# Eleven taps of the second block's depthwise convolution go to ScalarE and GpSimd

## The chip, the cores and the metric

One core of one Trainium2 chip runs the whole program. The metric is device time in microseconds (us) for one execution, inputs and outputs in device memory. TensorE (PE) multiplies matrices, VectorE (DVE), ScalarE (ACT) and GpSimd (POOL) work elementwise, SyncE (SP) issues most transfers. Each engine works its instructions off in a fixed order and waits on semaphores for the others.

## What is computed

Two transformer blocks on 512 tokens of width 1024, in float32. The second block ("block 2") projects its normalised input once, and among other things feeds a Conformer convolution and a sparse attention ("NSA"), whose outputs are concatenated:

```python
def conformer_conv(a, b, w_dw, b_dw, ln_g, ln_b):
    u = a * jax.nn.sigmoid(b)
    y = lax.conv_general_dilated(
        u, w_dw[:, None, :], window_strides=(1,), padding=[(CONV_KERNEL - 1, 0)],
        dimension_numbers=('NWC', 'WIO', 'NWC'), feature_group_count=CONV_WIDTH_2)
    y = layernorm(y + b_dw, ln_g, ln_b)
    return jax.nn.silu(y)
...
    y_conv = conformer_conv(conv_a, conv_b, ...)
    y_nsa = nsa_mixer(q, k_c, v_c, k_s, v_s, k_w, v_w, gate_logits, ...)
    h = h + jnp.concatenate([y_conv, y_nsa], axis=-1) @ w_out[l]
    h = h + memory_attention(...)
    h = h + peer(...)
```

The convolution is depthwise and causal: each of 512 channels has its own 31 weights ("taps"), and output token t is the sum over d = 0 to 30 of weight(30 - d) times u(t - d). It runs over 4 channel groups of 128.

## The kernel before, in words

Activations lie transposed, channels on the 128 partitions and 512 tokens along the free dimension. A weight goes to TensorE as two halves: `load` (L165) brings it by DMA (`raw`), ScalarE rounds it to the high half (`whi`, L181), VectorE subtracts to get the low half (`wlo`, L182). `mm3` (L213) makes three matmuls of each product (L216 to L218). `split` (L220) does the same high and low pair for activations (ScalarE L224, VectorE L225).

`mix2` (L919) is the stage of the change. Its first part, `front`, mixes several generators: `conv2_in` (L1009) projects one channel group j of the convolution and leaves u in `x[j]` (VectorE L1020, L1023 and L1024); `compress` (L1241) makes compressed keys and values of 32-token blocks; `nsa_kv` makes keys and values; `nsa_q` makes the queries, `x[4]` to `x[7]`. Keys and queries pass `rope` (L1074): ScalarE writes the high half `roph` (L224), VectorE the low half `ropl` (L225), TensorE multiplies both with a permutation (L1081, L1082), VectorE combines (`rops` L1084, then L1085, L1086). The second part runs `nsa` (scores, softmax, values), `memory_kv`, and what is left of the convolution, interleaved.

`conv2` (L1027) is the convolution of one group. It works in place on a buffer `cy`: the first tap is a `tensor_scalar` (L1033), the next 29 are one VectorE `scalar_tensor_tensor` each (L1035: shifted u times weight, plus `cy`), each followed by a `yield`; then ScalarE adds the bias (L1037) and VectorE the last tap, writing `x[j]` (L1038). The generator `taps` in `mix2` hands out one step of it per step of `front`, so that taps lie between other VectorE work. `conv2_norm` (L1041) needs all four groups.

The order on each engine is made when the program is built: the framework takes the instructions with their written order as priority and places them by its own estimate of durations. So a change of `conv2` shifts its neighbours on every engine too. Pools with a number of buffers (`bufs`) make a writer wait until the reader of the buffer's old content is done.

In the second half of `compress`, the tile `cX` has a single buffer: GpSimd clears its padding (L1268), then ScalarE and VectorE fill it (L224, L225), then TensorE multiplies (L1279, L1280).

Of the kernel before, what the change touches and what calls it, by code (L numbers as in the profile page):

```python
# [7 lines left out]
F32 = mybir.dt.float32  # L8
# [4 lines left out]
AF = mybir.ActivationFunctionType  # L13
OP = mybir.AluOpType
# [3 lines left out]
T = 512  # L18
# [5 lines left out]
MAGIC = 12582912.0  # L24

TD = 384
GS = 16
NGS = TD // GS

# [109 lines left out]
class Kern:  # L139
# [887 lines left out]
    def conv2(self, P, u, j):  # L1027

        nc = self.nc
        y = P.tile([128, T], F32R, name="cy", bufs=3).bitcast(F32)  # L1030
        cw = lambda i: self.v2(W_CW + j * 31 + i)
        nc.vector.memset(y[:, :1], 0.0)
        nc.vector.tensor_scalar(y[:, 1:], u[:, :T - 1], cw(29), None, op0=OP.mult)  # L1033
        for d in range(2, 31):
            nc.vector.scalar_tensor_tensor(y[:, d:], u[:, :T - d], cw(30 - d), y[:, d:], op0=OP.mult, op1=OP.add)  # L1035
            yield
        nc.scalar.activation(y, y, AF.Identity, bias=self.v2(W_CB + j))  # L1037
        nc.vector.scalar_tensor_tensor(u, u, cw(30), y, op0=OP.mult, op1=OP.add)  # L1038
        yield

# [473 lines left out]
    def peer(self):  # L1514
# [3 lines left out]

        self.gd = self.dp.tile([128, NGS, 128, GS], F32, name="gd")
        self.hd = [self.dp.tile([128, 8, TD], F32, name=f"hd{i}") for i in range(16)]  # L1520
        g = self.v2(W_PN, 8)
        with ExitStack() as es:
# [3 lines left out]

            hg = B.tile([128, 2, 8 * TD], F32, name="hg")
            lists = [{} for _ in range(4)]
# [6 lines left out]
            with ExitStack() as e1:  # L1535
# [20 lines left out]
                for n, _ in enumerate(hid):  # L1556
                    next(front, None)
                    for _ in range(1 + (n % 8 == 0)):
                        if done < TD // 4 and "T" in lists[1 + done // 32]:
                            next(gts)  # L1560
                            done += 1
                        elif done == TD // 4 and not pre:
                            pre = self.dense_load(hg, 0)
# [5 lines left out]
                for j in range(2):  # L1569
                    t = B.tile([128, 128, GS], F32, name="gst", bufs=2).rearrange("p k t -> p (k t)").bitcast(F32R)  # L1570
                    acts.append(self.dense_act(pre, j, t[:, :TD], t[:, TD:2 * TD]))
            with ExitStack() as e2:
# [195 lines left out]
    def gate_matrix(self, P, B, lists):  # L1768
# [3 lines left out]
        for n in range(0, TD, 4):  # L1772
            lt = lists[1 + n // 128]["T"]
            if n % GS == 0:
                st = B.tile([128, 128, GS], F32, name="gst", bufs=2)
            o1 = P.tile([128, 4, 128], F32, name="o1", bufs=2)
# [7 lines left out]
            for t in range(4):  # L1784
                nc.tensor.matmul(ps[:, t * 128:t * 128 + 128], o2[:, t], o1[:, t], start=True, stop=True)
            nc.scalar.activation(st[:, :, n % GS:n % GS + 4], ps.rearrange("p (t k) -> p k t", t=4), AF.Copy)
            if n % GS == GS - 4:
# [216 lines left out]
```

## Time and profile before

| | |
|---|---|
| three executions | 4443.55, 4454.96 (median), 4459.59 us |
| the profiled execution | 4446.65 us, of which the span is 4444.8 us |
| TensorE busy | 4278.3 us, 96% |
| VectorE busy | 2896.4 us, 65% |
| ScalarE busy | 2084.4 us, 47% |
| GpSimd busy | 474.1 us, 11% |
| convolution's taps, L1035 | 116 instructions, from 2624.9 to 2820.1 us |

The spans count from the start of the profiled execution. A share over the whole span is a mean over stages with different limits; the stage of the convolution is about 200 us of 4445. In the rows, PE is a matmul and PEld the weight load that overlaps it, and `cy` in a row is any buffer of that name.

### The profile page before, as it was taken

Reading aid. Unit: us, or ns where it says so; the run is one execution under the profiler, and the core shown is the slowest. Engines: PE = TensorE matmul, PEld = TensorE weight load, DVE = VectorE, ACT = ScalarE, POOL = GpSimd, SP = SyncE. Lnnn points to the kernel's source line nnn. Section 1 sums busy time; section 2 is a strip of 40 time slices with the busy share of each in tenths; the row PEclk is TensorE's granted clock in tenths of the full one; section 3 lists DMA queues with packets and bytes.
Section 4 is the critical chain, followed back from the end, with each engine's and each line's share of the span. In section 5 each row is a group of like instructions: output and inputs, shape, how many; then the busy total and the mean of one; then the engine's idle time right before and its main releaser. Section 6 shows DMA issues by size and latency. Waiting matters only on the chain. (4 is left out here: it accounts for less than half of the span.)

```text
span 4444.8 us, 57315 instructions
## 1 busy us (share of the span) xinstructions
PE 4278.3 (96%) x21268; PEld 3651.0 (82%) x21268; DVE 2896.4 (65%) x5563; ACT 2084.4 (47%) x3514; POOL 474.1 (11%) x399
## 2 busy tenths in 40 slices
PE   9999999999999999998999999899989999999999
PEld 7888887788888888887878877878889999877777
DVE  5346777553444448778563469855889987566666
ACT  4225776432232236776442234843437777333333
POOL 0000111000000001110000000000043232223322
PEclk9999999999999999999999999999999999999999
DMA  4233222522322232223872333422388999988885
GB/s 142 92 102 104 89 88 76 173 100 91 110 90 95 99 114 81 96 89 111 257 236 92 102 104 116 136 100 70 115 294 308 311 328 319 324 307 299 303 298 180
DMA packets 264104, 726.97 MB, mean 164 GB/s; under 512 B 24848, under 2 KB 92944, under 8 KB 258704
## 3 DMA queue, kind: packets, MB, share of 16 engines
q1 hardware_dynamic: 226960, 589.07, 39.5%
q0 software_dynamic: 36864, 134.23, 8.5%
q8 instruction: 167, 2.74, 0.2%
q14 instruction: 113, 0.93, 0.1%
HBM read 630.94 MB, written 92.27 MB: 163 GB/s over the span
## 5 line engine op out<-in xcount | busy, mean ns | idle before, releaser
L181 ACT ACTIVATE whi<-raw 128x1024 fp32r<-128x1024 f32 (+2 forms) x814 | 810.3, 996 | 1730.8 <-PE ps_a L217 860.4
L182 DVE TENSOR_TENSOR wlo<-raw,whi 128x1024 fp32r<-128x1024 f32 (+2 forms) x814 | 931.8, 1145 | 749.3 <-ACT whi L181 746.7
L216 PE MATMUL ps_a<-xh,whi 128*128 128x512 f32 x1808 | 708.5, 392 | 17.8 <-ACT xh L227 10.2
L217 PE MATMUL ps_a<-xl,whi 128*128 128x512 f32 x1808 | 707.1, 391 | 1.8 <-DVE xl L228 1.5
L218 PE MATMUL ps_a<-xh,wlo 128*128 128x512 f32 x1808 | 706.2, 391 | 0.0
L216 PEld LDWEIGHTS ps_a<-xh,whi 128*128 128x128 f32 x1808 | 341.1, 189 | 91.2 <-ACT xh L227 11.0
L216 PE MATMUL ps_H<-xh,whi 128*128 128x384 f32 (+1 forms) x1088 | 384.0, 353 | 23.0 <-ACT hid L1674 23.0
L217 PEld LDWEIGHTS ps_a<-xl,whi 128*128 128x128 f32 x1808 | 341.3, 189 | 73.8 <-DVE xl L228 2.9
L218 PEld LDWEIGHTS ps_a<-xh,wlo 128*128 128x128 f32 x1808 | 341.3, 189 | 71.4
L216 PE MATMUL ps_P<-xh,whi 128*128 128x512 f32 (+1 forms) x952 | 381.3, 401 | 12.4 <-DVE sq L511 4.2
L218 PE MATMUL ps_P<-xh,wlo 128*128 128x512 f32 (+1 forms) x952 | 376.5, 396 | 10.1 <-DVE wlo L182 10.1
L217 PE MATMUL ps_P<-xl,whi 128*128 128x512 f32 (+1 forms) x952 | 377.9, 397 | 0.0
L218 PE MATMUL ps_H<-xh,wlo 128*128 128x384 f32 (+1 forms) x1088 | 375.8, 346 | 1.0 <-DVE wlo L182 0.9
L217 PE MATMUL ps_H<-xl,whi 128*128 128x384 f32 (+1 forms) x1088 | 375.3, 345 | 0.0
L217 PE MATMUL ps_D<-wlo,gah 128*128 128x512 f32 x756 | 302.2, 400 | 22.2 <-DVE wlo L182 22.2
L216 PE MATMUL ps_D<-whi,gah 128*128 128x512 f32 x756 | 300.4, 397 | 6.7 <-ACT whi L181 6.6
L218 PE MATMUL ps_D<-whi,gal 128*128 128x512 f32 x756 | 299.3, 396 | 0.0
L216 PE MATMUL ps_a<-ah,whi 128*128 128x512 f32 x704 | 277.5, 394 | 0.0
L218 PE MATMUL ps_a<-ah,wlo 128*128 128x512 f32 x704 | 276.0, 392 | 0.0
L217 PE MATMUL ps_a<-al,whi 128*128 128x512 f32 x704 | 273.2, 388 | 0.0
L1797 POOL DMA_INDIRECT row<-in_pu_dram,ei x128 | 166.4, 1300 | 785.9 <-DVE tk L1510 389.7
L1797 POOL DMA_INDIRECT row<-in_pv_dram,ei x128 | 201.3, 1573 | 388.3 <-DVE y L1810 238.1
(545 smaller groups left out, 8048.5 us busy)
## 6 DMA issues: line engine op xcount, KB each, us to landing
raw<-in_up_dram SPq DMA_DIRECT2D x176, 512.0 KB
raw<-in_uT_dram SPq DMA_DIRECT2D x128, 512.0 KB
raw<-in_pv_dram SPq DMA_DIRECT2D x128, 512.0 KB
raw<-in_dn_dram SPq DMA_DIRECT2D x64, 704.0 KB
raw<-in_w_qkv_dram SPq DMA_DIRECT2D x48, 512.0 KB
hd<-hid SPq DMA_DIRECT2D x128, 192.0 KB
gd<-gst SPq DMA_DIRECT2D x24, 1024.0 KB
hg<-hd SPq DMA_DIRECT2D x16, 1536.0 KB
```

The lines of the kernel that those rows point to most:

```text
L181: nc.scalar.activation(hi[:, :m], t, AF.Copy)
L182: self.last = nc.vector.tensor_tensor(lo[:, :m], t, hi[:, :m].bitcast(F32), OP.subtract)
L216: mm(ps, wh, ah, start=start, stop=False)
L217: mm(ps, wh, al, start=False, stop=False)
L218: mm(ps, wl, ah, start=False, stop=stop)
L1797: nc.gpsimd.indirect_dma_start(out=r, out_offset=None, in_=src, in_offset=bass.IndirectOffsetOnAxis(ap=li["ei"][:, s:s + 1], axis=0))
```

## The change

Shifts 20 to 30, eleven taps of each group, leave VectorE's chain. ScalarE multiplies the shifted u by its weight (an `activation` Copy with a per-channel scale): the first product goes straight into a new buffer `cz`, the other ten into `czt`, which has two buffers. GpSimd clears the first 20 columns of `cz` and adds each `czt` to it, ten `tensor_tensor` per group. VectorE's chain keeps shifts 1 to 19, and gains one add of `cz` after the bias, before the last tap. A `conv2` now has 19 steps where it had 30, so that the generator ends sooner.

```diff
+FAR = 20
...
+        z = P.tile([128, T], F32, name="cz")
+        nc.gpsimd.memset(z[:, :FAR], 0.0)
+        nc.scalar.activation(z[:, FAR:], u[:, :T - FAR], AF.Copy, scale=cw(30 - FAR))
         nc.vector.memset(y[:, :1], 0.0)
         nc.vector.tensor_scalar(y[:, 1:], u[:, :T - 1], cw(29), None, op0=OP.mult)
-        for d in range(2, 31):
+        for d in range(2, FAR):
             nc.vector.scalar_tensor_tensor(y[:, d:], u[:, :T - d], cw(30 - d), y[:, d:], op0=OP.mult, op1=OP.add)
+            if FAR + d - 1 < 31:
+                s = FAR + d - 1
+                t = P.tile([128, T], F32, name="czt", bufs=2)
+                nc.scalar.activation(t[:, s:], u[:, :T - s], AF.Copy, scale=cw(30 - s))
+                nc.gpsimd.tensor_tensor(z[:, s:], t[:, s:], z[:, s:], OP.add)
             yield
         nc.scalar.activation(y, y, AF.Identity, bias=self.v2(W_CB + j))
+        nc.vector.tensor_tensor(y, y, z, OP.add)
         nc.vector.scalar_tensor_tensor(u, u, cw(30), y, op0=OP.mult, op1=OP.add)
```

In the changed file the lines of `conv2` are: product into `cz` L1037, tap L1041, product into `czt` L1045, GpSimd's add L1046, bias L1048, VectorE's add of `cz` L1049, last tap L1050. Lines above `conv2` move by 2, lines below it by 12.

The order moves at three places that matter below. First GpSimd, in the second half of `compress` (`cX` is the padding that TensorE's next product needs). Before:

```order
L1239 MEMSET QB 64x512
L1268 MEMSET cX 128x4x24
L1322 CAST kzh<-kch 64x2x32 x4
L1122 CAST V_21784<-V_21784 128x4x64
L1122 CAST V_21814<-V_21814 128x4x64
```

Now:

```order
L1251 MEMSET QB 64x512
L1046 TENSOR_TENSOR cz<-czt,cz 128x491
L1046 TENSOR_TENSOR cz<-czt,cz 128x490
L1046 TENSOR_TENSOR cz<-czt,cz 128x489
L1046 TENSOR_TENSOR cz<-czt,cz 128x488
L1046 TENSOR_TENSOR cz<-czt,cz 128x487
L1046 TENSOR_TENSOR cz<-czt,cz 128x486
L1046 TENSOR_TENSOR cz<-czt,cz 128x485
L1046 TENSOR_TENSOR cz<-czt,cz 128x484
L1046 TENSOR_TENSOR cz<-czt,cz 128x483
L1046 TENSOR_TENSOR cz<-czt,cz 128x482
L1280 MEMSET cX 128x4x24
```

The clearing of `cX` now stands behind all ten adds of group 0.

Second ScalarE, where the keys are made (`vc` belongs to `compress`, `roph` is the keys' rope). Before:

```order
L224 ACTIVATE vc_21655<-kc 32x64 x2
L224 ACTIVATE vc_21661<-kc 32x64 x2
L181 ACTIVATE whi<-raw 128x192
L181 ACTIVATE whi<-raw 128x1024
L224 ACTIVATE roph<-cQ 128x512 x2
```

Now:

```order
L226 ACTIVATE vc_21694<-kc 32x64 x2
L1045 ACTIVATE czt<-x_64,wv 128x489
L1045 ACTIVATE czt<-x_64,wv 128x488
L1045 ACTIVATE czt<-x_64,wv 128x487
L1045 ACTIVATE czt<-x_64,wv 128x486
L183 ACTIVATE whi<-raw 128x192
L1045 ACTIVATE czt<-x_64,wv 128x485
L1045 ACTIVATE czt<-x_64,wv 128x484
L1045 ACTIVATE czt<-x_64,wv 128x483
L1045 ACTIVATE czt<-x_64,wv 128x482
L183 ACTIVATE whi<-raw 128x1024
L226 ACTIVATE roph<-cQ 128x512 x2
```

Eight products of group 1 (`x_64` is `x[1]`) now stand ahead of the keys' `roph`.

Third ScalarE, where the first two queries are made (`x_67` and `x_68` are `x[4]` and `x[5]`, `x_65` is `x[2]`). Before:

```order
L181 ACTIVATE whi<-raw 128x1024
L224 ACTIVATE roph<-x_67 128x512
L224 ACTIVATE roph<-x_68 128x512
L1236 ACTIVATE QQ<-x_67 64x512
L1161 ACTIVATE cX<-ps_S 128x512
```

Now:

```order
L183 ACTIVATE whi<-raw 128x1024
L226 ACTIVATE roph<-x_67 128x512
L1045 ACTIVATE czt<-x_65,wv 128x487
L1045 ACTIVATE czt<-x_65,wv 128x486
L1045 ACTIVATE czt<-x_65,wv 128x485
L1045 ACTIVATE czt<-x_65,wv 128x484
L226 ACTIVATE roph<-x_68 128x512
L1045 ACTIVATE czt<-x_65,wv 128x483
L1045 ACTIVATE czt<-x_65,wv 128x482
L1248 ACTIVATE QQ<-x_67 64x512
L1173 ACTIVATE cX<-ps_S 128x512
```

Four products stand between the two queries' `roph`; the product into `cz` and four more stand ahead of the first. At the third pair, `x[6]` and `x[7]`, the products of group 3 lie in the same way, and the last four stand ahead of the first softmax's exponential.

## Rows read from the trace of the kernel before

**Rows 1.** The page: each engine's busy time, share of the span, instructions.

```profile
PE 4278.3 (96%) x21268; PEld 3651.0 (82%) x21268; DVE 2896.4 (65%) x5563; ACT 2084.4 (47%) x3514; POOL 474.1 (11%) x399
```

**Rows 2.** Windows: length; busy us of PE, PEld, DVE, ACT, POOL; granted clock; DMA.

```profile
2625.00:2636.00 11.00, 10.62 (x63) 9.03 (x61) 10.52 (x15) 3.79 (x7) 0.18 (x1) 1.00 0.29 97
2636.00:2651.70 15.70, 6.86 (x35) 6.72 (x35) 15.42 (x42) 4.33 (x9) 1.85 (x4) 0.62 0.31 108
2651.70:2656.70 5.00, 4.84 (x14) 4.03 (x15) 4.84 (x13) 3.40 (x10) 0.00 (x0) 0.50 0.00 0
2656.70:2740.00 83.30, 79.80 (x386) 62.95 (x385) 81.13 (x125) 22.89 (x34) 2.53 (x5) 0.99 0.37 120
2740.00:2838.00 98.00, 89.69 (x638) 81.82 (x639) 89.85 (x253) 79.46 (x204) 3.12 (x6) 0.99 0.36 122
```

**Rows 3.** Tile `cy`: line, engine, operation, count: ns min/median/max, first and last start.

```profile
L1035 DVE SCALAR_TENSOR_TENSOR cy<-x,wv,cy x116: 639/730/754, 2624.9 to 2820.1; 128x510 f32<-128x510 f32 x4, 128x509 f32<-128x509 f32 x4, 128x508 f32<-128x508 f32 x4, 128x507 f32<-128x507 f32 x4
L1037 ACT ACTIVATE cy<-cy,wv x4: 707/710/722, 2669.9 to 2820.8; 128x512 f32<-128x512 f32 x4
L1057 DVE TENSOR_TENSOR cy<-cy,cQ x3: 681/684/686, 2832.8 to 2834.8; 128x512 f32<-128x512 f32 x3
```

**Rows 4.** Windows, instructions of L1035 alone: DVE busy us, count.

```profile
2624.00:2740.00 116.00, 57.67 (x80) 0.92 0.34 111
2740.00:2838.00 98.00, 25.68 (x36) 0.99 0.36 122
```

**Rows 5.** Lines L721 and L633: GpSimd's two-input product and its cast.

```profile
L721 POOL TENSOR_TENSOR sq<-sq,lg x16: 1288/1298/2143, 435.3 to 2068.8; 128x512 f32<-128x512 f32 x16
L633 POOL CAST KB<-KK x32: 602/612/963, 413.9 to 2045.6; 64x512 fp32r<-64x512 f32 x32
```

**Rows 6.** Timeline at 2068 us, VectorE, then GpSimd: start, length, operation.

```profile
2068.55 1.22 DVE L182 TENSOR_TENSOR wlo<-raw,whi 128x1024 fp32r<-128x1024 f32 x1
...
2068.78 2.14 POOL L721 TENSOR_TENSOR sq<-sq,lg 128x512 f32<-128x512 f32 x1 [22.56 <-DVE sq L720]
```

**Rows 7.** Timeline at 413 to 419 us, VectorE, then GpSimd.

```profile
414.16 1.11 DVE L553 SCALAR_TENSOR_TENSOR BL<-x,x,x 128x512 fp32r<-128x512 f32 x1
415.19 0.68 DVE L225 TENSOR_TENSOR vv<-ps_T,vv 128x512 fp32r<-128x512 f32 x1
415.90 1.05 DVE L630 TENSOR_TENSOR KK<-qk,KK 64x512 fp32r<-64x512 f32 x1
416.98 0.99 DVE L631 TENSOR_TENSOR QB<-qk,QQ 64x512 fp32r<-64x512 f32 x1
418.00 0.69 DVE L630 TENSOR_TENSOR KK<-qk,KK 64x512 fp32r<-64x512 f32 x1
...
413.94 0.78 POOL L633 CAST KB<-KK 64x512 fp32r<-64x512 f32 x1 [28.65 <-ACT KK L628]
...
416.47 0.96 POOL L633 CAST KB<-KK 64x512 fp32r<-64x512 f32 x1
```

**Rows 8.** Timeline of TensorE, four places; in brackets the idle time before.

```profile
2638.83 0.37 PE L1279 MATMUL ps_T<-cX,whi 128*128 128x136 f32 x1 [3.20 <-DVE cX L225]
2651.75 0.42 PE L216 MATMUL ps_P<-whi,dvh 128*128 128x64 f32 x1 [6.07 <-ACT dvh L224]
...
2667.64 0.50 PE L1081 MATMUL ps_T<-roph,permr 128*128 128x512 f32 x1
...
2712.41 0.45 PE L1081 MATMUL ps_T<-roph,permr 128*128 128x512 f32 x1
...
2738.72 0.74 PE L1185 MATMUL ps_S<-KK,QQ 128*128 128x512 f32 x1 [0.94 <-DVE rops L1084]
```

**Rows 9.** Timeline of ScalarE at 2711 and 2740 us.

```profile
2711.68 0.63 ACT L224 ACTIVATE roph<-x 128x512 fp32r<-128x512 f32 x1 [2.68 <-PE ps_S L218]
...
2740.83 0.69 ACT L350 ACTIVATE p<-ps_S,nm 128x512 f32<-128x512 f32 x1 [2.42 <-DVE nm L349]
```

**Rows 10.** Waits of TensorE from 2740 to 2838 us: total, times, longest.

```profile
PE ps_S L1185 <- ACT p L350: 5.0, 8, 1.4
```

## The prediction

> **What bounds the kernel now.** The page comes first: TensorE is busy for 96% of the span, every other engine far less [rows 1]. So only idle or slowed TensorE time can be won, and every new wait of TensorE is lost. A share of the whole span says nothing about the 200 us of the convolution, so the second view is the windows [rows 2]. From 2625 to 2740 us VectorE is busy for 10.52, 15.42, 4.84 and 81.13 us of 11.0, 15.7, 5.0 and 83.3: it is full. TensorE's idle time in these windows is 0.4 + 8.8 + 0.2 + 3.5 = 12.9 us, most of it in `compress`. From 2740 to 2838 us VectorE still has 89.85 of 98 and TensorE idles for 8.3, of which 5.0 are score matmuls that wait for the softmax's exponential [rows 2, 10]. The third view is the tile `cy`: 116 taps of 0.73 us [rows 3], 80 of them before 2740 us (57.67 us of VectorE) and 36 after (25.68 us) [rows 4]. So both engines are near their limit, and taps fill nearly half of VectorE's time up to 2740. What a lighter VectorE could win is at most those 21 us of idle TensorE and what its lower clock costs.
>
> **What the change takes off VectorE.** Eleven taps in each of four groups: 44 x 0.73 = 32.1 us less, and four adds of `cz` more, priced like L1057's add of the same size: 4 x 0.68 = 2.7 us [rows 3]. The net is 29.4 us. Counting taps in the new order up to the first softmax reduction gives 59 where it was 80, so 21 taps (15.3 us) go before 2740 and 23 (23 x 0.71 = 16.4 us) after.
>
> **ScalarE.** 44 products, no row of their own. The nearest row, a 512-column activation with a per-channel operand, takes 0.71 us [rows 3]; times 486/512, the mean width, that is 0.67, in all 29.7 us. ScalarE has 34.4 us of work in the 115 us before 2740 [rows 2], so by themselves they are covered. The cover goes when a product waits: `czt` has two buffers, so the third product waits for GpSimd's first add, and all that stands behind it on ScalarE waits too.
>
> **GpSimd.** 40 adds. The nearest row is its two-input product of 512 columns: 1.30 us [rows 5], so 1.23 for 486. It has little else to do. But one of those products took 2.14 us [rows 6]: it began at 2068.78 while VectorE ran a weight split of two SBUF inputs (2068.55 to 2069.77), and ended at 2070.92, so it was let in only when that was over, and then took 1.15. The other way round it looks the same: a cast of GpSimd that ended at 417.43 held a VectorE subtraction of two SBUF inputs, which ended at 417.97 and took 0.99, where the next of its kind took 0.69; a `scalar_tensor_tensor`, the taps' operation, took 1.11 at 414.16 beside the cast before; a VectorE instruction that reads PSUM took its usual 0.68 at 415.19 [rows 7]. So two-input VectorE work and GpSimd's reads take turns. Taps, weight splits and rope products are all two-input work, in long rows.
>
> The price of an add to VectorE, if it holds back for its whole length: 1.15 x 486/512 = 1.09 us, less the 0.15 by which a held instruction is shorter once let in (0.54 against 0.69) = 0.94. **From below** it is bounded by what the cast does, 0.48 (416.95, the end of VectorE's instruction at 415.90, to 417.43) less 0.15 = 0.33, and by zero if an add holds nothing; **from above** by the full 1.23. I take 0.94: a two-input instruction was let in only after VectorE's, and that is the same pair in the other order. No row shows a two-input add holding up a tap.
>
> The Trainium skill speaks of just this on its page "SBUF — State Buffer", section "Who interferes with whom": a VectorE instruction with two SBUF inputs contends with any GpSimd instruction that reads SBUF, and whichever starts first has the shared port for its whole length. By that rule the price is the 0.94 and not the 0.33; the trace agrees as far as the cast and the held product go (0.99 for 0.69, 2.14 for 1.30).
>
> **Where TensorE waits for it.** Four places, one per group, each read from the order:
>
> 1. *Group 0, before `compress`'s second product.* Its padding is cleared behind all ten adds, and VectorE must pass eleven taps and two weight splits (as many as before) in turn with them: 10 x 0.94 = 9.4 us later. Two drains of about 0.7 us each have moved behind, so 8.0. TensorE has nothing else there: it began at 2638.83, after waiting 3.20 for VectorE [rows 8].
> 2. *Group 1, before the keys' rope.* ScalarE's `roph` stands behind eight products, VectorE's drains of the keys behind nine taps and ten adds: 9.4, less three instructions of 0.73 fewer than before = 7.2. TensorE multiplied with `roph` at 2667.64, at once [rows 8].
> 3. *Group 2, before the second query's rope.* `roph` waits for the sixth add: 6 x 0.94 = 5.6. It was written at 2711.68 and used at 2712.41 [rows 8, 9].
> 4. *Group 3, before the first scores.* Seven adds fall between the queries' rope instructions: 7 x 0.94 = 6.6. The scores began at 2738.72 and the first exponential at 2740.83 [rows 8, 9]; that one also stands behind the last four products.
>
> Together 27.4 us. A check from VectorE's whole load: 40 x 0.94 = 37.6 more, 15.3 less, three adds of `cz` 2.0 more, is 24.3 on an engine without slack.
>
> **Clock.** Behind a wait of 6.07 us [rows 8] TensorE was busy for 4.84 of 5.0 us at a granted clock of 0.50, its 1.2 GHz level [rows 2]: half of that, 2.4 us, is lost. Place 1 lies where the clock is low already (0.62). For the other three the bounds are 0 and 7.2; I take 3, since matmuls break these waits up.
>
> **After 2740 us.** VectorE is relieved by 16.4 us. TensorE can win back its 8.3 at the most, nothing at the least; I take 4, because ScalarE, at 79.46 of 98, stays in the softmax chain. `conv2_norm` comes earlier in the order, at the same cost. Cost at nothing: GpSimd's clearing of `cz` (20 columns), the added `yield`s that fall away, and `V`'s casts behind group 1's adds, which are read only after 2740.
>
> **Sum:** 27.4 + 3 - 4 = 26 us. Against the profiled execution's own 4446.65 that is 4473; the median of the three runs is 8.3 us above that one, so 4454.96 + 26 = **4481 us**, 0.6% more.
>
> **Rivals.**
> - *The adds hold VectorE only as long as a cast does.* With 0.33 the places come to 1.9 + 1.1 + 2.0 + 2.3 = 7.3, the clock to about 1, and 4 come back: +4; with places 3 and 4 still paced by ScalarE's waits for `czt`, up to +15. I give +8, 4463. For it: the only row with a held VectorE instruction has a one-input cast. Against it: the 2.14.
> - *Faster.* Adds and taps run side by side, and VectorE is truly 29 us lighter. Half of TensorE's 21.2 us of idle time then goes: -10, 4445. It decides whether a tap beside an add stays at 0.73. Against it stand [rows 6, 7].
> - *ScalarE becomes the bound after 2740.* Group 3's products run on past the first exponential; some 10 us of them and of delayed softmax work on an engine at 81% cost about 10 more than the forecast: +36, 4491.
> - That the change moves nothing is ruled out by the order of the program.
>
> **Chances.** Forecast (+15 to +35) 0.55, cast-like hold 0.27, faster 0.08, ScalarE bound 0.10. About 0.5%, here 22.3 us, is what a measurement of this kernel can tell from no change. The forecast lies above that in three of four parts, the ScalarE case wholly: 0.41 + 0.10 = 0.51 slower; the faster case passes 22 us only if nearly all idle time goes: 0.03; the rest, 0.46, the same. The range goes from 4450 (-5, below the cast-like hold) to 4498 (+43: all upper bounds of the clock and the last rival) and leaves out most of the faster case. The forecast's own range is 4470 to 4490.
>
> **What would show it.** Right: taps and weight splits from 2625 to 2750 that take up to 1.8 us instead of 0.73 and 1.22; GpSimd's adds at 1.7 to 2 us instead of 1.23; `compress`'s second product about 8 us later, the keys' `roph` about 15, the first scores about 27; low clock behind these waits. Wrong: taps at 0.73 beside adds; TensorE's idle time between 2625 and 2740 below the present 12.9 us; or the first scores late by far less than VectorE is.

## The result and the profile after

The changed kernel takes 4487.12 us in the median of 6 runs (4477.1 to 4497.63), the kernel before 4448.62 beside it; the ratio is 1.008, with a 95% interval of 1.0066 to 1.0094. So it is slower: by 36 us going by the ratio, by 38.5 between the two medians. The forecast was +26 us and 4481 us; the time lies inside the range of 4450 to 4498, in its upper part. The profiled execution has a span of 4486.4 us, 41.6 more than that of before.

Each engine's busy time on the page of the changed kernel [rows 1]:

```profile
PE 4293.9 (96%) x21268; PEld 3665.2 (82%) x21268; DVE 2904.3 (65%) x5523; ACT 2114.9 (47%) x3558; POOL 531.9 (12%) x443
```

It tells almost nothing: TensorE is at 96% as before. The windows do [rows 2]:

```profile
2625.00:2636.00 11.00, 11.00 (x66) 9.66 (x65) 10.31 (x10) 6.81 (x9) 6.51 (x4) 1.00 0.05 11
2636.00:2651.70 15.70, 4.92 (x23) 4.09 (x22) 15.52 (x18) 7.12 (x12) 10.01 (x8) 0.75 0.30 101
2651.70:2656.70 5.00, 4.88 (x24) 4.74 (x23) 5.00 (x13) 2.64 (x5) 0.00 (x0) 0.50 0.32 107
2656.70:2740.00 83.30, 67.15 (x309) 53.49 (x310) 69.06 (x100) 34.96 (x59) 32.40 (x28) 0.85 0.23 77
2740.00:2838.00 98.00, 83.22 (x491) 70.35 (x490) 86.41 (x197) 64.25 (x147) 20.48 (x18) 0.91 0.34 113
```

From 2656.7 to 2740 us TensorE is busy for 67.15 us where it was 79.80, at a granted clock of 0.85 where it was 0.99. VectorE is full until 2656.7 us as before, and has 69.06 us of 83.3 after it where it had 81.13. What left it is gone, but some of what stayed got longer. The taps in the tile `cy` reach 1.761 us where they reached 0.754 [rows 3]; their median is as before, for 15 of the 72 take over 1.5 us and most of the others 0.7. GpSimd's adds in the tile `cz` take 1.546 us in the median:

```profile
L1041 DVE SCALAR_TENSOR_TENSOR cy<-x,wv,cy x72: 650/736/1761, 2628.0 to 2816.2; 128x510 f32<-128x510 f32 x4, 128x509 f32<-128x509 f32 x4, 128x508 f32<-128x508 f32 x4, 128x507 f32<-128x507 f32 x4
```

```profile
L1046 POOL TENSOR_TENSOR cz<-czt,cz x40: 1202/1546/2096, 2629.3 to 2774.7; 128x491 f32<-128x491 f32 x4, 128x490 f32<-128x490 f32 x4, 128x489 f32<-128x489 f32 x4, 128x488 f32<-128x488 f32 x4
```

How they stand to each other is in the timelines at 2629 us, VectorE first, then GpSimd (start, length, operation):

```profile
2629.60 1.62 DVE L1041 SCALAR_TENSOR_TENSOR cy<-x,wv,cy 128x508 f32<-128x508 f32 x1
2631.25 1.61 DVE L1041 SCALAR_TENSOR_TENSOR cy<-x,wv,cy 128x507 f32<-128x507 f32 x1
2632.79 2.27 DVE L184 TENSOR_TENSOR wlo<-raw,whi 128x1024 fp32r<-128x1024 f32 x1
...
2668.14 5.24 DVE L227 TENSOR_TENSOR vc<-kc,vc 32x64 fp32r<-32x64 f32 x4
```

```profile
2629.25 1.42 POOL L1046 TENSOR_TENSOR cz<-czt,cz 128x491 f32<-128x491 f32 x1 [13.94 <-ACT czt L1045]
2630.75 1.58 POOL L1046 TENSOR_TENSOR cz<-czt,cz 128x490 f32<-128x490 f32 x1
2632.40 1.57 POOL L1046 TENSOR_TENSOR cz<-czt,cz 128x489 f32<-128x489 f32 x1
2634.05 2.09 POOL L1046 TENSOR_TENSOR cz<-czt,cz 128x488 f32<-128x488 f32 x1
```

Strict turns: the tap that begins at 2629.60 waits for the add of 2629.25, which ends at 2630.67, and ends 0.55 us after it; the next add waits for that tap, and so on. A tap takes 1.62 in place of 0.73, a split 2.27 in place of 1.22, and an add 1.55 in place of 1.23. The smallest instruction pays the same: four subtractions of 32 x 64 elements, of 0.2 us each before, took 5.24 us together behind four adds.

Now the four places [rows 8], TensorE's timeline with the idle time in brackets:

```profile
2649.54 0.48 PE L1291 MATMUL ps_T<-cX,whi 128*128 128x136 f32 x1 [10.78 <-DVE cX L227]
...
2686.57 0.79 PE L1093 MATMUL ps_T<-roph,permr 128*128 128x512 f32 x1 [7.97 <-ACT roph L226]
...
2738.11 0.51 PE L1093 MATMUL ps_T<-roph,permr 128*128 128x512 f32 x1 [1.04 <-ACT roph L226]
...
2774.30 0.80 PE L1197 MATMUL ps_S<-KK,QQ 128*128 128x512 f32 x1 [3.87 <-ACT cX L1173]
```

Beside before's 2638.83, 2667.64, 2712.41 and 2738.72 these are 10.7, 18.9, 25.7 and 35.6 us later. But 3.1 us of each are older than the convolution: at 2600 us the profiled execution was already that much behind, though no instruction ahead of it is changed. With the offset at 2600 us taken off, the four matmuls are late by **7.6, 15.8, 22.6 and 32.5 us**. The same count, for every kernel that was run, is the table on which the rest is argued: offsets in us against the kernel before at the four places and at 2882.52 us of before, at the first matmul of the projection behind the softmax stage, each less the kernel's own offset at 2600 us. Matmuls are matched by their place in TensorE's order.

| kernel | place 1 | place 2 | place 3 | first scores | 2882 |
|---|---|---|---|---|---|
| the change | 7.6 | 15.8 | 22.6 | 32.5 | 38.9 |
| e5_no_helper | 0.0 | 0.2 | 0.2 | 0.9 | 6.7 |
| e1_short_adds | -0.9 | -0.1 | 0.6 | 1.5 | 7.4 |
| e2_adds_alone | 8.8 | 19.5 | 22.8 | 37.0 | 42.4 |
| e6_psum_sum | 3.1 | 5.7 | 6.5 | 16.8 | 25.4 |
| f1_no_helper_late | 0.0 | 0.6 | 0.6 | 1.3 | 0.5 |
| f2_norm_late | 7.6 | 15.8 | 22.4 | 32.3 | 31.7 |
| f3_psum_late | 2.6 | 4.9 | 3.7 | 14.1 | 15.7 |
| f5_spread | 7.6 | 15.8 | 22.5 | 32.4 | 37.9 |
| e4_cx_vector | 7.1 | 15.8 | 22.7 | 32.6 | 39.0 |
| g15_before_late | 0.0 | 0.0 | 0.0 | 0.1 | 1.6 |
| g35_before_late | 0.0 | 0.3 | 0.3 | 0.8 | 5.3 |

These are from one execution each. How well they repeat is shown by f5, which turned out to be the same order of instructions as the change (below): it agrees to 0.1 us at the four places and to 1.0 us at 2882, far better than whole times do.

### The profile page after: what moved, and what is told of

It is laid out like the page before. It is cut to its first block, busy times and chain, and to the rows that moved or that the text cites. A ratio compares the mean times of both kernels' runs of the same rounds, so it can differ in the third digit from the quotient of the medians.

```text
span 4486.4 us, 57389 instructions
## 1 busy us (share of the span) xinstructions
PE 4293.9 (96%) x21268; PEld 3665.2 (82%) x21268; DVE 2904.3 (65%) x5523; ACT 2114.9 (47%) x3558; POOL 531.9 (12%) x443
## 5 line engine op out<-in xcount | busy, mean ns | idle before, releaser
L218 PE MATMUL ps_a<-xh,whi 128*128 128x512 f32 x1808 | 709.4, 392 | 18.6 <-ACT xh L229 12.5
L218 PEld LDWEIGHTS ps_a<-xh,whi 128*128 128x128 f32 x1808 | 341.5, 189 | 92.0 <-ACT xh L229 13.3
L218 PE MATMUL ps_H<-xh,whi 128*128 128x384 f32 (+1 forms) x1088 | 385.2, 354 | 22.6 <-ACT hid L1686 22.6
```

Source lines behind the costliest of these rows:

```text
L218: mm(ps, wh, ah, start=start, stop=False)
```

## The experiments

Two questions stood open: is it the adds that cost the time, and by which way; and why is what should come back after 2740 us (-4 forecast) a loss of 6.4 (38.9 - 32.5)?

### What a lighter VectorE is worth: e5_no_helper

The edit is shown against the change:

```diff
-        z = P.tile([128, T], F32, name="cz")
...
         for d in range(2, FAR):
             nc.vector.scalar_tensor_tensor(y[:, d:], u[:, :T - d], ...)
-            if FAR + d - 1 < 31:
...
-        nc.vector.tensor_tensor(y, y, z, OP.add)
```

> The eleven taps of each group are left out and nothing takes their place, so the sum lacks them; VectorE has 32 us less to do, ScalarE and GpSimd nothing more. Theory (a lighter VectorE is worth something, and the adds eat it up by holding VectorE): TensorE's 21.2 us of idle time between 2625 and 2838 us of the kernel before shrink by a half to all of it, 4425 to 4440 us. Rival (VectorE is not what TensorE waits for, so the change could never win): 4445 to 4452 us.

Measured: 4453.63 us (11 runs) against 4443.48, ratio 1.0021 (1.001 to 1.0032). Taking 44 taps off VectorE and putting nothing in their place makes the kernel slower by 10 us. The theory that relief is worth something fell, and even the rival, which allowed no gain, ended at 4452 and had no room for so large a loss. The table splits it: nothing is won before the first scores (0.9), and 6 us are lost in the softmax stage.

### Products without long adds: e1_short_adds

```diff
-                nc.gpsimd.tensor_tensor(z[:, s:], t[:, s:], z[:, s:], OP.add)
+                nc.gpsimd.tensor_tensor(z[:, s:s + 8], t[:, s:s + 8], z[:, s:s + 8], OP.add)
```

> The change with GpSimd's 40 adds cut to 8 columns each, so that most of those products are not summed; ScalarE's 44 products stay whole and still wait for the adds. Theory (the adds' length on the shared way to SBUF is what costs): the adds fall to some 0.2 us or less, taps stay at 0.73 us, and the time falls to 4428 to 4448 us. Rival (ScalarE's 30 us of products stand in front of the splits and of the rope's first half): 4465 to 4487 us.

Measured: 4446.31 us (11 runs) against 4443.48, ratio 1.0008 (0.9994 to 1.0022): no difference that can be measured, and inside the theory's range (the adds were to take some 0.2 us or less, though, and took 0.581 in the median). (`conv2_norm` moves up here as in e5, and the table's one execution shows its 5.9 us between the first scores and 2882; of that the whole times show less.) Its taps, and its adds of 8 columns:

```profile
L1041 DVE SCALAR_TENSOR_TENSOR cy<-x,wv,cy x72: 650/736/750, 2625.4 to 2782.3; 128x510 f32<-128x510 f32 x4, 128x509 f32<-128x509 f32 x4, 128x508 f32<-128x508 f32 x4, 128x507 f32<-128x507 f32 x4
```

```profile
L1046 POOL TENSOR_TENSOR cz<-czt,cz x40: 201/581/1270, 2626.6 to 2740.3; 128x8 f32<-128x8 f32 x40
```

The longest tap is 0.75 us. VectorE's busy time on the page, for as many instructions, is 2874.8 us where the change has 2904.3, so the length of the 40 adds costs VectorE 29.5 us. All 44 products are on ScalarE, in front of splits and rope, and the first scores come 1.5 us late: the products by themselves cost next to nothing.

### Adds without products: e2_adds_alone

```diff
         nc.scalar.activation(z[:, FAR:], u[:, :T - FAR], AF.Copy, scale=cw(30 - FAR))
+        t = P.tile([128, T], F32, name="czt", bufs=2)
+        nc.scalar.activation(t, u, AF.Copy, scale=cw(0))
...
-                t = P.tile([128, T], F32, name="czt", bufs=2)
-                nc.scalar.activation(t[:, s:], u[:, :T - s], AF.Copy, scale=cw(30 - s))
```

> The change with GpSimd's 40 adds whole, but one product per group that is added ten times in place of ten products, so that ScalarE waits for no add; the sum is another one. Theory (adds hold VectorE): taps next to adds stay at 1.6 us, the wait before compress's second product stays some 7 us longer than before, places 3 and 4 lose what ScalarE's waits put on top: 4462 to 4480 us. Rival (the time is lost because ScalarE waits for the two product buffers with the rope behind it): 4435 to 4452 us.

Measured: 4478.92 us (5 runs) against 4443.48, ratio 1.0079 (1.0062 to 1.0096): the whole loss of the change, though no product waits for an add. (The clearing of `cX` behind the ten adds still does: ScalarE waits 9.5 us for it, where it waits 1.7 in the change.) The kernel's waits of TensorE from 2629 to 2790 us (total, times, longest):

```profile
PE ps_T L1291 <- DVE cX L227: 11.9, 1, 11.9
PE ps_T L1093 <- ACT roph L226: 10.1, 3, 8.5
PE ps_P L218 <- ACT dvh L226: 6.4, 2, 6.1
PE ps_T L1094 <- DVE ropl L227: 5.9, 4, 2.0
```

`roph` is still late, though of the helper only two products per group are left on ScalarE: what it is made from comes late, and the keys' first `roph` waits 8.5 us for VectorE's `cQ`. The time is in the theory's range, but its step that places 3 and 4 would be less late without ScalarE's waits did not come true: they are 22.8 and 37.0 us late, and at places 1, 2 and 4 this kernel is even later than the change. Why was not tried apart.

### Is it two operands in SBUF: e6_psum_sum

```diff
-        y = P.tile([128, T], F32R, name="cy", bufs=3).bitcast(F32)
+        y = self.ps("a") if j < 3 else P.tile([128, T], F32R, name="cy", bufs=3).bitcast(F32)
```

> The change with VectorE's running sum of groups 0 to 2 kept in one bank of PSUM instead of SBUF; all else as in the change. The taps then read one operand from SBUF and one from PSUM. Theory (the hold is between GpSimd's reads of SBUF and VectorE instructions with two operands in SBUF): in these groups taps stay at 0.73 to 0.85 us beside adds of 1.25 us, only weight splits are still held, and the time is 4450 to 4472 us; one bank makes a group's first tap wait for the end of the group before, which may give some of it back. Rival (any VectorE instruction beside a GpSimd add is held): taps at 1.6 us as in the change, 4480 to 4492 us.

Measured: 4467.51 us (5 runs) against 4443.48, ratio 1.0046 (1.003 to 1.0062), inside the theory's range. Its taps on the PSUM bank, with the first one of a group (L1039), and its adds:

```profile
L1041 DVE SCALAR_TENSOR_TENSOR ps_a<-x,wv,ps_a x54: 719/742/754, 2631.5 to 2750.3; 128x510 f32<-128x510 f32 x3, 128x509 f32<-128x509 f32 x3, 128x508 f32<-128x508 f32 x3, 128x507 f32<-128x507 f32 x3
L1039 DVE TENSOR_SCALAR ps_a<-x,wv x3: 752/753/753, 2630.7 to 2716.5; 128x511 f32<-128x511 f32 x3
```

```profile
L1046 POOL TENSOR_TENSOR cz<-czt,cz x40: 1203/1245/2302, 2632.4 to 2768.4; 128x491 f32<-128x491 f32 x4, 128x490 f32<-128x490 f32 x4, 128x489 f32<-128x489 f32 x4, 128x488 f32<-128x488 f32 x4
```

The taps are the same, and the adds run beside them as in the change, yet none of the 54 taps takes over 0.754 us, while the adds fall from 1.546 to 1.245 in the median. What the edit changes is where one operand of the tap lies (in one PSUM bank, which the three groups share, in place of three SBUF buffers). At place 3 the kernel is late by 6.5 us where the change was by 22.6. The VectorE instructions that are still held have both operands in SBUF: weight splits of up to 2.0 us, the small subtractions in `vc` and rope instructions. From place 3 to the first scores the kernel loses 10.3 us, as the change does (9.9), and there it is not by group 3's taps, which stay in SBUF: two of the 18 take 1.1 us and the others some 0.73. Three of the rope's instructions (L1097 and L1098) meet group 3's adds and take 1.70 to 1.72 us in place of 0.68; in the change three take 1.69 to 1.71.

### Where the loss after 2740 us comes from: f1_no_helper_late and f2_norm_late

The filler that advances the taps goes on to `conv2_norm` when they are done. With 44 taps fewer it has 44 steps fewer, and `conv2_norm` moves up into the softmax by some 40 us (its first drain starts at 2794.4 us in e5, whose offset is 5.8 us, and at 2829.4 before). Both kernels give the steps back, empty, f1 to e5_no_helper and f2 to the change:

```diff
         nc.vector.scalar_tensor_tensor(u, u, cw(30), y, op0=OP.mult, op1=OP.add)
         yield
+        if j == 3:
+            for _ in range(44):
+                yield
```

> The eleven taps are left out and nothing takes their place, as in e5_no_helper, but 44 empty steps follow the fourth group's taps, so that conv2_norm comes at the step at which it came before the change. Theory (the lighter VectorE itself is worth nothing to TensorE, and e5's 10 us are lost because conv2_norm moves up into the softmax): 4437 to 4447 us, and TensorE's offset against the kernel before stays within 2 us up to 2742 us and within 3 us at 2882 us. Rival (the 10 us come from somewhere else): 4450 to 4456 us.

> The change with 44 empty steps after the fourth group's taps, so that conv2_norm comes at the step at which it came before; all else as in the change. Theory (the term after 2740 was of the wrong sign because conv2_norm moved up, and the rest of the loss is the adds'): 4474 to 4482 us. Rival (what is lost after 2740 comes from the last group's adds and products): 4484 to 4490 us.

Measured: f1 4445.86 us (12 runs) against 4444.4, ratio 1.0007 (0.9994 to 1.002); f2 4473.64 (6 runs), ratio 1.0067 (1.0046 to 1.0088). f1 is as the theory has it; f2 lies 0.4 us below the theory's range of 4474 to 4482. Whole times alone would not carry the point, since the interval of f2 overlaps that of the change, and f1's that of e5; the table does. In it, the softmax stage now costs f2 -0.6 (32.3 to 31.7) where it cost the change 6.4, and f1 -0.8 where it cost e5 5.8. The waits of TensorE in that stage show by what. The change from 2820 to 2930 us, then f2 from 2815 to 2890:

```profile
PE ps_P L218 <- DVE x L678: 5.8, 1, 5.8
PE ps_S L1197 <- ACT p L352: 4.7, 9, 1.0
PE ps_P L218 <- DVE cQ L1436: 3.7, 1, 3.7
```

```profile
PE ps_S L1200 <- ACT p L352: 3.2, 6, 1.2
...
PE ps_P L218 <- ACT cQ L1437: 0.3, 1, 0.3
```

A projection of `memory_kv` waits 3.7 us for the drain of its result into a `cQ` buffer. `conv2_norm` takes its temporaries from the same five `cQ` buffers and stands on ScalarE and VectorE at that moment: VectorE's drain begins at 2843.85 us, directly behind an instruction of `conv2_norm` (L1083) that had waited 0.96 for ScalarE:

```profile
2843.24 0.69 DVE L1083 SCALAR_TENSOR_TENSOR x<-cQ,x 128x512 f32<-128x512 f32 x1 [0.96 <-ACT x L1082]
2843.85 0.68 DVE L1436 TENSOR_TENSOR cQ<-ps_P,R 128x512 f32<-128x512 f32 x1
```

Whether the shared buffers or the engines' order hold the drain was not tried apart. The 5.8 us are the wait of the projection behind the softmax for `x`, at which the column 2882 is taken; it is 3.8 in the trace of before and 3.3 in that of f2.

And f1 gives the answer to the question on which the forecast rested. Its window of the first 115 us, beside 111.91 us of VectorE and 102.12 of TensorE before [rows 2, summed]:

```profile
2629.80:2744.80 115.00, 101.39 (x492) 81.58 (x491) 98.58 (x172) 35.34 (x60) 4.58 (x10) 0.91 0.33 111
```

VectorE is freed of 13.3 us there, and TensorE's busy time is within 0.8 us of what it was.

### Attempts at a better version: f5_spread, f3_psum_late, e4_cx_vector

f5 was to spread the ten products and adds of a group over every second tap:

```diff
-            if FAR + d - 1 < 31:
-                s = FAR + d - 1
+            if d % 2 == 0 or d == 19:
+                s = FAR + (d // 2 if d < 19 else 10)
```

> The change with its ten products and adds of a group spread over every second tap instead of one behind each of the first ten; the running sums stay in SBUF. Theory (each add holds VectorE for its length wherever it stands, so only ScalarE's waits shrink): 4472 to 4484 us, taps beside adds 1.6 us, ten of them per group as before. Rival (the loss comes from ScalarE's waits for the product buffers, which spreading takes away): 4445 to 4460 us.

Measured: 4480.36 us (6 runs) against 4444.4, ratio 1.0081 (1.0062 to 1.0099), inside the theory's range, with the change's offsets to 0.1 us at all four places. But the edit changed only the written order. In the two traces the four compute engines work off the same instructions in the same order (TensorE's 21268 matmuls, and 5523, 3558 and 443 instructions of VectorE, ScalarE and GpSimd): the framework placed the adds where it had placed them before, ten in a row per group, and ScalarE's products wait for them for 26.1 us in 30 waits in both. So f5 is a repetition of the change. It decides neither whether it matters where the adds stand among the taps nor what ScalarE's waits cost; on the latter there is only e2, which loses as much without them.

f3 joins what seemed to help: the sums of groups 0 to 2 in PSUM (as e6), `conv2_norm` at its old step (as f2), the written order of f5 with three product buffers, and the padding of `cX` cleared on VectorE. The lines that it shares with f2 and f5 are shown there.

```diff
-        y = P.tile([128, T], F32R, name="cy", bufs=3).bitcast(F32)
+        y = self.ps("a") if j < 3 else P.tile([128, T], F32R, name="cy", bufs=3).bitcast(F32)
...
-                t = P.tile([128, T], F32, name="czt", bufs=2)
+                t = P.tile([128, T], F32, name="czt", bufs=3)
...
-            nc.gpsimd.memset(X[:, :, :, 256:].bitcast(F32), 0.0)
+            nc.vector.memset(X[:, :, :, 256:].bitcast(F32), 0.0)
```

> The change with VectorE's sum of groups 0 to 2 in PSUM, conv2_norm at its former step, the ten products and adds spread over every second tap with three product buffers, and the padding of cX cleared on VectorE. Theory: the taps are not held, ScalarE's queue does not wait for adds, the weight splits alone are held at times: 4440 to 4455 us, no slower than before by more than 0.3%. Rival (with VectorE lighter nothing is to be won, and what the adds still hold costs all the same): 4455 to 4468 us.

Measured: 4457.24 us (12 runs) against 4444.4, ratio 1.0028 (1.0017 to 1.0039): the best version with a helper, two thirds of the change's loss gone, and still slower than before; the theory's range is missed by 2 us and the rival's holds. Its waits of TensorE from 2700 to 2790 us:

```profile
PE ps_T L1096 <- ACT roph L226: 5.0, 4, 1.8
PE ps_S L1200 <- ACT cX L1176: 2.3, 1, 2.3
...
PE ps_T L1097 <- DVE ropl L227: 1.6, 2, 1.1
```

The rope of group 3's stretch is most of what is left, 10.4 us between place 3 and the first scores; three of its instructions take 1.7 us beside the adds, as in e6.

e4 is the change with the padding of `cX` alone on VectorE:

```diff
-            nc.gpsimd.memset(X[:, :, :, 256:].bitcast(F32), 0.0)
+            nc.vector.memset(X[:, :, :, 256:].bitcast(F32), 0.0)
```

> The change with the padding of cX cleared on VectorE instead of GpSimd, where it stood behind the ten adds of group 0; all else as in the change. Theory (place 1 is late because VectorE comes to the split of cX late, past its held taps and weight splits): compress's second product starts within 1.5 us of the change's offset, which is 7.6 us later than before, counted from the offset at 2600 us. Rival (place 1 is late because the clearing waits behind the adds): that offset falls by 3 us or more.

Measured in one execution of 4485.25 us: 7.1 us at place 1 where the change has 7.6. VectorE's timeline there:

```profile
2646.98 5.65 DVE L1041 SCALAR_TENSOR_TENSOR cy<-x,wv,cy 128x503 f32<-128x503 f32 x4
2652.60 0.14 DVE L1280 MEMSET cX<- 128x96 f32 x1
...
2653.07 0.68 DVE L227 TENSOR_TENSOR cX<-cy,cX 128x512 fp32r<-128x512 f32 x1
```

The split of `cX` is reached behind four taps that take 5.65 us together, where four of 0.73 would take 2.9, wherever the clearing stands. In the change itself GpSimd's clearing ends at 2646.48 us, and VectorE reaches that split only at 2648.71:

```profile
2646.31 0.17 POOL L1280 MEMSET cX<- 128x96 f32 x1
...
2648.71 0.69 DVE L227 TENSOR_TENSOR cX<-cy,cX 128x512 fp32r<-128x512 f32 x1
```

### Is `conv2_norm` already at its best place: g15_before_late and g35_before_late

Both are the kernel before, with no tap moved, and 15 or 35 of f1's empty steps.

```diff
+        if j == 3:
+            for _ in range(15):
+                yield
```

> The kernel before, with 15 empty steps after the fourth group's taps, so that conv2_norm comes later than it did; no tap is moved. Theory (44 steps earlier cost 8 to 10 us because conv2_norm shares the cQ buffers and ScalarE with the softmax and the memory projections, and that cost still falls at its place of before): 4 us less, 4438 to 4443 us. Rival (its place of before is already out of the way): 4443 to 4448 us.

> The kernel before, with 35 empty steps after the fourth group's taps, which puts conv2_norm at the end of the softmax stage; no tap is moved. Theory (later is cheaper): 4436 to 4442 us. Rival (at the end it stands in front of the output projection, which needs its result, and costs more than it frees): 4446 to 4456 us.

Measured: 4446.53 us (12 runs) against 4447.14, ratio 1.0001 (0.9988 to 1.0014), and 4448.41 us (11 runs), ratio 1.0012 (1.0002 to 1.0023). Later wins nothing, and g35 is even slower by a little; the rivals hold. No version that was run beats the kernel before.

## Why the prediction was right, and where it was not

**The price of an add, 0.94 us: right.** The held taps at 2629.60 and 2631.25 take 0.89 and 0.88 more than 0.73, the split at 2632.79 1.05 more than 1.22. The cast-like hold of 0.33 is out: taps reach 1.761 us. Not every add met a two-operand instruction, though: against e1 the 40 adds cost VectorE 29.5 us in all, 0.74 each, where the check from VectorE's load took 37.6. And GpSimd's adds took 1.55 us in the median, where 1.7 to 2 was named as a sign. The rule of the Trainium skill's page "SBUF — State Buffer", section "Who interferes with whom", gave the better price; its other half, that a VectorE instruction with at most one SBUF input, outside the modes that use both ports, does not contend, is what e6 shows with its 0.754 at most.

**Place 1, 8.0 us: 7.6.** But one of its two causes was idle: the forecast named the clearing behind ten adds and VectorE's taps and splits in turn with them, and e4 shows that the second alone sets it.

**Place 2, 7.2 us: 8.2** (15.8 - 7.6). **Clock, 3 us: 2.4 in the open.** Behind place 2 TensorE was busy for 42.2 of 42.8 us, at a mean granted clock of 0.94 from 2686.6 to 2729.4 us; the matmul that stood at 2708.10 before starts at 2729.40, 18.2 us late after the offset, 2.4 more than at place 2. A slower stretch lies inside place 4, at a granted clock of 0.58 from 2760 to 2780 us, so part of what place 4 shows is the clock's. **Place 3, 5.6: 4.4** (22.6 - 18.2). **Place 4, 6.6: 9.9** (32.5 - 22.6), under-sized; how much of the excess is held rope instructions and how much the clock was not taken apart. The sum at the first scores was to be 30.4 with the clock and is 32.5.

**After 2740 us, -4: +6.4, the step that failed.** Two sentences were wrong. The first, "`conv2_norm` comes earlier in the order, at the same cost", priced a moved step at nothing because its own instructions do not change; f2 against the change shows 7.2 us at 2882 (38.9 - 31.7). The second took a relieved VectorE for time won: f1 gives TensorE at most 0.8 us back of 8.3. They make 10.4 of the 12.5 us by which the forecast's sum of 26.4 falls short of 38.9. That 4481 is nevertheless only 6 us below 4487 is luck: the sum was put on 4454.96, the median of three executions of the kernel before, and the median of the six is 4448.62.

**"What a lighter VectorE could win is at most those 21 us": true, and no more than a bound.** f1 shows that it is nothing. Half of VectorE's 111.91 of 115 us of work was taps (57.67 us [rows 4]), and they fill the gaps between the instructions that TensorE waits for. With a quarter of the taps away those instructions came no sooner; that this is because they wait for TensorE, for ScalarE and for each other in turn is argued here and not shown. But where held taps and splits stand in front of one of them, it comes later: ten held instructions of about 0.9 us put off place 1 by 7.6.

**The rivals.** The cast-like hold and the faster case are out by the taps' times. The case in which ScalarE becomes the bound after 2740 gave 4491, near what was measured, but not by its mechanism: with all products in place and `conv2_norm` put back (f2) nothing is lost after the first scores, and with two products per group in place of eleven (e2) nearly as much is lost there as with them (5.4 against 6.4).

## What to carry to other kernels

An engine that is 97% busy is not the bound if its work is filler: leave the moved work out altogether, with everything else at its place, before building a helper for it; here that experiment gives nothing to win. Here each VectorE instruction with two operands in SBUF that met one of GpSimd's adds of 1.23 us took 0.9 to 1.1 us longer, even one of 0.2 us; taps with one operand in PSUM did not, but other instructions on the path, the rope's, were still held. A change of the written order is an experiment only if the order on the engines changes: compare it in the trace (f5). When a generator that other work is interleaved with gets shorter, look at what follows it: it moves up, and here that cost a fifth of the loss.

## What was not expected of the hardware

Turns are taken per instruction, not per element: in e1 GpSimd's adds of 8 columns took 0.581 us in the median and 0.201 at the least, so that most of them waited for a tap, and in the change the subtractions of 32 x 64 took 1.3 us each behind an add, where others of the same size take 0.2. And the first product of a group, a `tensor_scalar` of 511 columns, took 0.753 us into PSUM (e6, groups 0 to 2, above) where the same instruction takes 0.48 into SBUF. Of group 3 in e6:

```profile
L1039 DVE TENSOR_SCALAR cy<-x,wv x1: 482/482/482, 2748.6 to 2748.6; 128x511 f32<-128x511 f32 x1
```
